# Which engine waits for the last stores: the final wait moved from SyncE to TensorE

## The chip, the cores and the metric

One core of one Trainium2 chip. The metric is the device time of one execution in microseconds (us), called the counted time where it stands beside the profiler's span of the same execution. A semaphore is a counter: in the traces here stores raise `stored` (three stores, 48 landings on semaphore 114), one instruction takes it down (159.633 us in the kernel before), and the kernel's waits test it. All runs told here are of the fast state, with a granted clock of 1.0.

## The reference

```python
def reference(x):                      # x: 32 x 512 x 1024 float32
    relu_x = np.maximum(x, 0)
    return np.sum(relu_x, axis=-1).astype(np.float32)
```

67 MB are read, 64 KB are written.

## The kernel before

The body streams the input through three buffers. ScalarE and VectorE clamp and sum, and SyncE issues every load and store. The last store carries two columns of results; each store raises the semaphore `stored` by 16 (the trace has 48 landings on it, the last at 159.599 us). What comes after the body:

```python
    n_stores = relu_sum(nc, sems, x, out)
    body.extend(ends)
    # ... (cut)
    nums = sorted(s.num for s in (*sems.loads, sems.act, sems.dve))
    cleared = range(nums[0], nums[-1] + 1)
    assert len(cleared) == len(nums)
    nc.sync.sem_clear(cleared)
    nc.sync.wait_ge(sems.stored, 16 * n_stores).then_inc(sems.stored, -16 * n_stores)
```

```python
    def store(m, n, act, dve):
        # ... (cut)
        nc.sync.wait_ge(sems.act, act)
        nc.sync.dma_start(out=dst, in_=src).wait_op(sems.dve, dve, "sem-ge").then_inc(
            sems.stored, 16
        )
        n_store += 1
```

So SyncE issues the third store (at 158.20 us), clears the semaphores of the body (99 to 113, at 158.57) while it flies, waits until `stored` (semaphore 114) is 48 (the last landing, 159.599), takes it down to zero (159.633), and leaves the program.

## Time and profile before

| | before |
|---|---|
| device time, first three runs | 161.35 us median (161.24 to 161.53) |
| the profiled execution, counted time | 160.99 us |
| its span, first to last instruction of the program | 159.63 us |
| its last store landed at | 159.599 us |

The page's span and the counted time are not the same thing: 1.36 us of the counted time lie after the program's last instruction. That stretch has no line in the page. It can be read only from the trace's record of semaphore updates.

### The profile page before, as it was taken

The page shows a single profiled execution, that of the slowest core. Times are in us where ns is not written, and L with a number is a line of the kernel's source. Part 1 is how long each engine was busy: PE and PEld are TensorE (multiplying, and loading weights), DVE is VectorE, ACT ScalarE, POOL GpSimd, SP SyncE. Part 2 cuts the span into 40 slices and gives each one's busy share as a digit, 9 for nine tenths or more (in the row PEclk, how much of TensorE's full clock was granted, in tenths as well). Part 3 has the DMA queues.
Part 4 walks back from the last instruction along what each step waited for, and adds up shares of the span by engine and source line. Part 5 has one row for each costly group of instructions (what it writes and reads, how often), then busy time and mean ns, then how long its engine had stood idle before and what let it go on. Part 6 is the DMA issues. An engine that isn't in the chain of part 4 may idle for free.

```text
span 159.6 us, 129 instructions
## 1 busy us (share of the span) xinstructions
DVE 117.5 (74%) x41; ACT 104.2 (65%) x50; POOL 0.2 (0%) x4
## 2 busy tenths in 40 slices
DVE  0000000009999499994999999999999999999986
ACT  3000059990799708996099941999339992499985
POOL 0000000000000000000000000000000000000000
DMA  7996996996996998979969969969969969798994
GB/s 263 525 525 263 525 526 263 525 525 263 526 493 296 525 411 378 525 328 460 526 279 509 525 263 526 525 263 525 525 263 525 509 279 525 337 452 386 412 405 127
DMA packets 2304, 67.18 MB, mean 421 GB/s; under 512 B 640, under 2 KB 896, under 8 KB 1024
## 3 DMA queue, kind: packets, MB, share of 16 engines
q1 hardware_dynamic: 2304, 67.18, 98.1%
HBM read 67.11 MB, written 0.07 MB: 421 GB/s over the span
## 4 chain that ended last, share of the span: by engine, by line
DMA 43%; DVE 34%; ACT 17%; another core or an unknown queue 3%; SPq 0%; issue 0%; DVEq 0%
DMA io<-in_x_dram 43%; DVE res L123 32%; ACT io L115 17%; DVE io L140 1%; SPq L97 0%; DVE piece L219 0%; DVE piece L140 0%; DVEq L218 0%
## 5 line engine op out<-in xcount | busy, mean ns | idle before, releaser
L123 DVE TENSOR_REDUCE res<-io 128x8 f32<-128x8192 f32 (+2 forms) x9 | 101.1, 11286 | 39.9 <-ACT io L115 39.9
L115 ACT ACTIVATE io<-io 128x8192 f32<-128x8192 f32 (+2 forms) x9 | 81.7, 9111 | 46.9 <-DMA io<-in_x_dram 46.9
L130 ACT ACTIVATE io<-io 128x1024 f32<-128x1024 f32 x20 | 20.9, 1045 | 5.9 <-DMA io<-in_x_dram 5.7
L140 DVE TENSOR_SCALAR_CACHE_REDUCE io<-io 128x1024 f32<-128x1024 f32 (+1 forms) x14 | 15.5, 1165 | 0.7 <-DMA io<-in_x_dram 0.6
L130 ACT ACTIVATION_READ_ACCUMULATOR io<-io 128x1 f32 x20 | 3.8, 188 | 0.0
L115 ACT ACT_TABLE_LOAD x1 | 1.3, 1283 | 0.8 <-PEq L260 0.8
L140 DVE DVE_READ_ACCUMULATOR io<-io 128x1 f32 x14 | 1.2, 82 | 0.0
L219 DVE TENSOR_SCALAR_CACHE_REDUCE piece<-piece 128x406 f32<-128x406 f32 x1 | 0.6, 576 | 0.1
L140 DVE TENSOR_SCALAR_CACHE_REDUCE piece<-piece 128x260 f32<-128x260 f32 x1 | 0.4, 424 | 0.0
L260 POOL MEMSET const-bfloat16-1.0<- 128x1 bf16 x1 | 0.1, 102 | 0.0
L260 POOL MEMSET const-uint8-127<- 128x1 uint8 x1 | 0.1, 102 | 0.0
L260 POOL MEMSET const-float32-0.0<- 128x1 f32 x1 | 0.1, 99 | 0.2 <-issue 0.2
L260 POOL MEMSET const-float32-1.0<- 128x1 f32 x1 | 0.1, 99 | 0.0
L140 DVE DVE_READ_ACCUMULATOR piece<-piece 128x1 f32 x1 | 0.1, 83 | 0.0
L219 DVE DVE_READ_ACCUMULATOR piece<-piece 128x1 f32 x1 | 0.1, 82 | 0.0
## 6 DMA issues: line engine op xcount, KB each, us to landing
io<-in_x_dram SPq DMA_DIRECT2D x1, 4096.0 KB, 21.6
io<-in_x_dram SPq DMA_DIRECT2D x1, 2048.0 KB, 26.1
io<-in_x_dram SPq DMA_DIRECT2D x1, 1204.0 KB, 28.6
io<-in_x_dram SPq DMA_DIRECT2D x1, 512.0 KB, 29.4
piece<-in_x_dram SPq DMA_DIRECT2D x1, 202.0 KB, 29.3
piece<-in_x_dram SPq DMA_DIRECT2D x1, 130.0 KB, 29.3
io<-in_x_dram SPq DMA_DIRECT2D x7, 26.9
out_dram<-res SPq DMA_DIRECT2D x1, 55.0 KB, 1.6
```

What stands on the lines that cost most here:

```text
L115: i = nc.scalar.activation(out=ap, in_=ap, func=RELU)
L123: nc.vector.tensor_reduce(out=res[:, m : m + n], in_=ap, axis=mybir.AxisListType.X, op=ADD).wait_op(sems.act, n_act, "sem-ge").then_inc(se ...
L130: i = nc.scalar.activation(out=ap, in_=ap, func=RELU, accum_out=res[:, m : m + 1])
L140: i = nc.vector.tensor_scalar(out=ap, in0=ap, scalar1=0.0, scalar2=None, op0=MAX, op1=ADD, accum_out=accum_out,)
L219: nc.vector.tensor_scalar(out=last[:, :], in0=last[:, :], scalar1=0.0, scalar2=None, op0=MAX, op1=ADD, accum_out=res[:, NT - 2 : NT - 1],) ...
L260: nc = _bacc.Bacc("TRN2", target_bir_lowering=False, num_devices=1)
```

## The change

The wait and the decrement move to TensorE, which has no busy line in this kernel's page. The apparent intent is that SyncE can go on to its own closing work while the last store is still in flight.

```diff
     nc.sync.sem_clear(cleared)
-    nc.sync.wait_ge(sems.stored, 16 * n_stores).then_inc(sems.stored, -16 * n_stores)
+    nc.tensor.wait_ge(sems.stored, 16 * n_stores).then_inc(sems.stored, -16 * n_stores)
     issue_ahead_of_the_barrier(tc, EARLY)
```

## The prediction

> **What bounds the kernel now.** I read the head of the page first, then the chain of work that ended last.
>
> ```profile
> span 159.6 us, 129 instructions
> DVE 117.5 (74%) x41; ACT 104.2 (65%) x50; POOL 0.2 (0%) x4
> q1 hardware_dynamic: 2304, 67.18, 98.1%
> HBM read 67.11 MB, written 0.07 MB: 421 GB/s over the span
> ...
> DMA 43%; DVE 34%; ACT 17%; another core or an unknown queue 3%; SPq 0%; issue 0%; DVEq 0%
> ```
>
> The reader is to see that the DMA engines are busy 98.1% of the span: the body is a stream of 67 MB, with VectorE and ScalarE behind it. TensorE has no busy line at all. The change touches no load, no arithmetic and no store, so I leave the body and look only at what follows the last arithmetic. The timeline gives the end of that, the list of DMA issues the flight of the last store, the DMA queue's own waits the wait that the change moves:
>
> ```profile
> 157.58 0.58 DVE L219 TENSOR_SCALAR_CACHE_REDUCE piece<-piece 128x406 f32<-128x406 f32 x1
> 157.62 0.19 ACT L130 ACTIVATION_READ_ACCUMULATOR io<-io 128x1 f32 x1
> 158.09 0.08 DVE L219 DVE_READ_ACCUMULATOR piece<-piece 128x1 f32 x1
> ...
> out_dram<-res SPq DMA_DIRECT2D x1, 1.0 KB, 1.4
> ...
> SPq L46 <- SPq L46: 1.0, 1, 1.0
> ...
> L46 SPq EVENT_SEMAPHORE  x1: 17/17/17, 159.6 to 159.6; - x1
> ```
>
> VectorE ends at 158.17 us; SyncE issues the last store at 158.20 (333 ns); that 1 KB lands 1.4 us after its issue. L46 is the wait for the stores; SyncE stands in it 1.0 us, it runs at 159.6, and with it the span ends. (L45, the clearing of the other semaphores, ran at 158.6 for 57 ns, beside the store's flight.) So after the last arithmetic the order is: store issue, flight of the store, wait released, end.
>
> The time that counts is longer than the span. The profiled execution has 160.99 us by the device and a span of 159.63: 1.36 us lie after the program's own last instruction. The trace also records every semaphore update[...]. In us from the span's start:
>
> ```
> semaphore 114 (stores)   last landing 159.599, taken down by SyncE 159.633
> semaphore 2, entering    1.003  157.912  157.950  158.313  159.764
> semaphore 2, returning   159.807 159.845 159.880 159.926
> semaphores 207-255 reset from 159.896, 156-206 from 159.946, 105-155 from 159.986,
>             54-104 from 159.990, 3-53 (first recorded is 7) from 160.140 to 160.488
> semaphore 2, second time 160.752 .786 .825 .869 .892 .990 161.028 .062 .109
> ```
>
> Semaphore 2 is passed along the engines and back. The late entries fit engine by engine the last update of each: ScalarE 157.812 then 157.912 (+100 ns), VectorE 158.180 then 158.313 (+133), SyncE 159.633 then 159.764 (+131). The one at 1.003 must be an engine that was done by then: TensorE (its one update at 0.784, +219) or GpSimd. I take TensorE as the first in line, because the block 3 to 53 is reset last and with a lag of about 0.19 us after its release, as long as the lag at 1.003. That is an inference; the record doesn't name the engine. Then the line is TensorE, ScalarE, GpSimd, VectorE, SyncE, and back. The sixth entry of the second round, 160.990 us, equals the device time of this execution, so I believe that the counted time ends inside this second round and everything that delays the first round is counted.
>
> [...]
>
> **The change part by part.** *Removed from SyncE:* a wait and decrement of 17 ns. SyncE still issues the store and clears 99 to 113, and then enters the closing line at about 158.63 + 0.13 = 158.76 instead of 159.764. This looks like a gain of 1 us but isn't: the line can't close before the store has landed, on whichever engine waits. *Added on TensorE:* the same wait. It sets no earlier release: the landing stays at 159.599.
>
> *Cost of one event-semaphore on TensorE.* The opening barrier shows it for both engines:
>
> ```profile
> L260 SPq EVENT_SEMAPHORE  x1: 17/17/17, 0.7 to 0.7; - x1
> ...
> L260 PEldq EVENT_SEMAPHORE  x1: 51/51/51, 0.7 to 0.7; - x1
> ```
>
> 51 ns against 17; from start to recorded update 63 against 18, so +45 ns. Landing to decrement was 34 ns on SyncE, so about 79 on TensorE: 159.678.
>
> *Leaving the program.* SyncE needed 131 ns from that update to its entry, TensorE 219 (0.784 to 1.003): entry at 159.897, against SyncE's 159.764.
>
> *The way through the line.* Before, the late engine was the one at the turn: only the four returning hops were left, 43 + 38 + 35 + 46 = 162 ns, and TensorE was released at 159.926. Afterwards the late engine is the first: four entering hops, 34 + 39 + 44 + 23 = 140 ns by the second round, then the turn at VectorE[...] (98 ns in the second round, 111 in an earlier one, against 43 where it had been waiting), then 38 + 34 + 47 = 119. With about 105 for the turn it is 140 + 105 + 119 = 364 ns: release at 159.897 + 0.364 = 160.261.
>
> *Sum.* 160.261 − 159.926 = +0.335 us, of it 45 for the slower instruction, 88 for the slower exit, 202 for the longer way. From there on TensorE resets its block, alone at the end, and opens the second round, before as after: nothing absorbs the delay. 161.35 + 0.335 = 161.69 us. I shade it to 161.65, because TensorE's 219 ns at the start need not repeat: with SyncE's 131 the sum is +0.25.
>
> **The rivals.**
> (a) *It gets faster by having SyncE free earlier.* This is probably the intent: the idle engine takes the wait, and SyncE's own closing work (its block 207 to 255) goes on early. Against it: SyncE's reset starts only when the line has turned at it (159.896, after its entry at 159.764), its block is done by 160.006, while block 3 to 53 ends at 160.488; SyncE isn't the last. If the order of the line were the other way round, TensorE would sit at the turn, and only 45 + 88 = +0.13 us would remain: 161.5.
> (b) *The counted time ends with SyncE's own last instruction plus a constant.* Then it falls by about a microsecond (SyncE's last instruction at 158.63 instead of 159.63): 160.35, −0.6%. For it: the metric is not defined in the profile. Against it: the 1.36 us after the span match an entry of the second round to the nanosecond, and that round needs all engines.
> (c) *TensorE, asleep since 0.8 us, wakes slowly or must fetch its next instructions.* [...] Against it: in the opening barrier it woke 13 ns after SyncE, and after a stand of 159 us in the closing line it began its reset within about 0.19 us.
> (d) *All hidden*: 161.35. Against it: in the first round nothing runs after the landing but the chain itself.
>
> **Range and chances.** The three runs before lie within 0.29 us (161.24 to 161.53), as much as the expected effect. Low end 161.35: the reversed line or a shorter exit, with a favourable draw. High end 161.95: the full sum with a slow wake and an unfavourable draw. A 2% verdict needs 3.2 us; even rival (b) gives a third of that. So within 2%: 0.98, and 0.01 on each side.
>
> **What would show it.** In the changed kernel's profile the wait's instruction should stand under PEldq with about 51 ns near 159.65, the span should be about the same or some 0.05 us longer, and SyncE's list should end with the clear at about 158.6. Among the semaphore updates three late entries should follow one at about 159.90 in hops of about 40 ns instead of standing at 157.9 to 158.3, and block 3 to 53 should begin about 0.33 us later after the last landing. If the counted time falls by a microsecond, rival (b) holds and I have the metric's end wrong; if late entries still stand at 157.9 and 158.3, I have the line's order wrong; if the wait starts well over 0.1 us after the last landing, it is (c).

The marks in this text stand for statements that no trace of this case shows. What the trace of the kernel before does show:

- Semaphore 2 is named by none of the program's 129 instructions. Its updates after the body, and the resets of the other semaphores, which come in five stretches of numbers (207, 156, 105, 54 and 3 upward), are called the closing sequence here; whose work it is the record doesn't say. That block 207 to 255 is SyncE's and block 3 to 53 TensorE's is inferred from the order in which they are reset.
- In the second round, nine updates again like the first, the hops are 23 to 47 ns, and the turn is 98. Why the turn takes 43 ns in the first round and 98 in the second isn't shown.
- The listing gives the wait's own instruction, not the time stood in it: SyncE stood 1.0 us at L46, which shows 17 ns.
- On rival (c): TensorE's event-semaphore is slower than the others' (51 ns against 17 to 21), and so is the exit taken to be its own (219 ns against 100 to 133). Its drain in the opening barrier is not: 8 ns, against 8 on ScalarE, 10 on VectorE, 132 on SyncE and 181 on GpSimd.

## The result, and the profile after

| | before | after |
|---|---|---|
| device time, six runs each | 161.34 us (161.16 to 161.53) | 161.61 us (161.48 to 161.84) |
| ratio of the fast runs | | 1.0018, interval 1.0005 to 1.0031 |
| the profiled execution, counted time | 160.99 us | 161.56 us |
| its last landing | 159.599 us | 159.814 us |
| counted time after the last landing | 1.391 us | 1.746 us |

A ratio is the mean time of one kernel's fast runs over that of the other's of the same rounds, so it is not quite the ratio of the medians. By it the changed kernel is about 0.29 us slower, which is "same" at the 2% level but clear of zero.

The page of the changed kernel, its head, its busy times and its DMA queue:

```profile
span 159.9 us, 129 instructions
...
DVE 117.5 (73%) x41; ACT 104.2 (65%) x50; POOL 0.2 (0%) x4
...
q1 hardware_dynamic: 2304, 67.18, 97.9%
```

The same number of instructions, the same busy times, the same bytes on this queue: the body was not touched. (This page also has one packet of 24 bytes on the queue of instructions, at 0.14 us; the kernel before has one like it 0.08 us ahead of its span.) The listing of the wait's own line, L46, and of the clear's, L45, in the changed kernel:

```profile
L46 PEldq EVENT_SEMAPHORE  x1: 51/51/51, 159.8 to 159.8; - x1
...
L45 SPq EVENT_SEMAPHORE_RANGE_CLEAR  x1: 58/58/58, 158.8 to 158.8; - x1
```

The wait now stands on TensorE's sequencer and shows 51 ns where SyncE's showed 17. The list of the DMA queue's own waits, changed kernel:

```profile
SPq L97 <- DVE res L123: 123.1, 5, 51.5
SPq L107 <- ACT io L130: 28.2, 2, 27.3
SPq L108 <- DVE piece L219: 0.3, 1, 0.3
SPq L260 <- PEq L260: 0.2, 1, 0.2
```

The line "SPq L46 <- SPq L46: 1.0, 1, 1.0" is gone, and nothing stands in its place in the lists of waits, this one or that of the engines. It is the same in the experiments below where the wait stands on ScalarE, GpSimd or VectorE, so it isn't that TensorE is idle; why the lists leave it out was not looked into. A reader of that list alone would book a gain of 1 us. In the DMA issues of the changed kernel the last store takes as long as before:

```profile
out_dram<-res SPq DMA_DIRECT2D x1, 1.0 KB, 1.4
```

The packet records split these 1.4 us: in the kernel before, 0.83 us pass from the start of the issue to the first packet, the packets take 0.20 us, and the last landing comes 0.38 us after the last packet; in the changed kernel it is 0.83, 0.20 and 0.37 us.

The semaphore record of the two executions shows where the time went. Times are in us from the span's start; "entering" and "returning" are the updates of semaphore 2, called the closing line:

```
                  before                                  after
last landing      159.599                                 159.814
114 taken down    159.633  (+34 ns)                       159.906  (+92)
entering          1.003 157.912 157.950 158.313 159.764   160.125 .159 .198 .242 .265
returning         159.807 .845 .880 .926                  160.363 .401 .435 .482
3-53 reset until  160.488                                 161.045
second round      160.752 .786 .825 .869 .892             161.310 .344 .383 .427 .450
                  .990 161.028 .062 .109                  .548 .586 .620 .667
counted time      160.990                                 161.560
```

Before, four engines had entered the line by 158.313 and only SyncE was late. After, nobody could enter until TensorE had, at 160.125, and the other four followed in hops of 34, 39, 44 and 23 ns. From the last landing to the last return it is 327 ns before and 668 ns after, 341 ns more. From that return to the opening of the second round it is 826 ns before and 828 after: nothing is made up.

The two profiled executions differ by 0.57 us in counted time, more than the kernels do. Of this, 0.215 us is a later last landing. The spans of the nine runs before in the first group of experiments lie between 159.7 and 159.9 us, so part of it at least is the variation of the body from run to run, and I don't read it as an effect of the change. The quantity free of it is the counted time after the last landing: 1.391 against 1.746 us.

That is one execution of each, but the record can check it on all. It gives every execution's time, and its span to 0.1 us. Time less span is 1.63 to 1.71 us in the six executions of the changed kernel, and 1.33 to 1.42 us in the 29 executions of the kernel before that were timed beside the experiments. The two ranges don't touch. (The span ends with the wait's own instruction, at 159.632 and 159.895 us in the two profiled executions, so this difference leaves out the few hundredths of a microsecond by which the semaphore is taken down later.)

### The profile page after: what moved, and what is told of

The parts are those of the page before. It is cut to its first block, busy times and chain, and to the rows that moved or that the text cites. A ratio compares the mean times of both kernels' runs of the same rounds, so it can differ in the third digit from the quotient of the medians.

```text
span 159.9 us, 129 instructions
## 1 busy us (share of the span) xinstructions
DVE 117.5 (73%) x41; ACT 104.2 (65%) x50; POOL 0.2 (0%) x4
## 4 chain that ended last, share of the span: by engine, by line
DMA 44%; DVE 33%; ACT 17%; another core or an unknown queue 3%; SPq 1%; issue 0%
DVE res L123 32%; DMA io<-in_x_dram 25%; DMA piece<-in_x_dram 18%; ACT io L115 17%; SPq L97 1%; DVE piece L219 0%
```

## The experiments

Each kernel gave the right result. In the tables, "landing to return" is from the last landing of a store to the last return of the closing line's first round, split in three: until the late engine has taken its semaphore down, until it has entered the line, and until the line has come back. It was 34 + 131 + 162 = 327 ns in the kernel before. "Tail" is the counted time after the last landing, less the 1.391 us of before.

### The wait on each of the engines

Edit, with `tensor`, `scalar`, `gpsimd` and `vector` in turn:

```diff
-    nc.sync.wait_ge(sems.stored, 16 * n_stores).then_inc(sems.stored, -16 * n_stores)
+    nc.scalar.wait_ge(sems.stored, 16 * n_stores).then_inc(sems.stored, -16 * n_stores)
```

Expected:

> The changed kernel again, on the chip where the next three run. Place theory (the late engine's place in the closing line counts, besides its own speed): from the last landing of a store to TensorE's release from the first round about 668 ns as in the first trace after, against 327 before; counted time +0.34 us (first result: +0.27 by the medians). Engine theory (TensorE's own slower instruction and exit are all of it, 45 + 88 ns, and the rest was chance): +0.13 us.

> ScalarE waits. Place theory (second in line): landing to decrement 34, exit 100, hops 39 + 44 + 23, turn 98, back 38 + 34 + 47: landing to last release about 457 ns, so +0.13 us. Engine theory: its exit of 100 ns against SyncE's 131 makes it -0.03 us. In the semaphore record the GpSimd, VectorE and SyncE entries should follow the late one, with one entry (TensorE) at about 1.0 us alone.

> GpSimd waits. Place theory (third in line): 34, an exit never seen alone, guessed as 131, hops 44 + 23, turn 98, back 119: about 449 ns, +0.12 us (up to +0.21 if its exit is as slow as TensorE's). Engine theory: about 0. In the record two entries, at about 1.0 us and after ScalarE's end, stand before the late one.

> VectorE waits. Place theory (fourth): 38, exit 133, hop 23, turn 98, back 119: about 411 ns, +0.08 us. Engine theory: about +0.01 us. In the record three early entries, then the late one and SyncE 23 ns behind it.

Measured, against 161.19 us for the kernel before on this chip (nine runs, 161.07 to 161.27):

| the wait is on | time, us | ratio (interval) | landing to return, ns | against before | tail, us |
|---|---|---|---|---|---|
| TensorE | 161.55 | 1.0024 (1.0011 to 1.0037) | 92 + 219 + 357 = 668 | +341 | +0.35 |
| ScalarE | 161.42 | 1.0015 (1.0001 to 1.0029) | 45 + 132 + 323 = 500 | +173 | +0.18 |
| GpSimd | 162.00 | 1.0046 (1.0034 to 1.0059) | 50 + 559 + 284 = 893 | +566 | +0.57 |
| VectorE | 161.33 | 1.0010 (0.9997 to 1.0022) | 58 + 172 + 243 = 473 | +146 | +0.16 |

Time less span, over all executions, is 1.65 to 1.70 us with TensorE, 1.50 to 1.53 with ScalarE, 1.90 to 1.98 with GpSimd and 1.48 to 1.54 with VectorE, against 1.33 to 1.42 for the nine of the kernel before. So the later end is in every execution, VectorE's too, and not in the profiled one alone.

The listing of L46 in the runs with the wait on TensorE's three alternatives, in the order GpSimd, VectorE, ScalarE, one fence each:

```profile
L46 POOLq EVENT_SEMAPHORE  x1: 17/17/17, 159.7 to 159.7; - x1
```

```profile
L46 DVEq EVENT_SEMAPHORE  x1: 21/21/21, 159.8 to 159.8; - x1
```

```profile
L46 ACTq EVENT_SEMAPHORE  x1: 17/17/17, 159.9 to 159.9; - x1
```

The instruction itself shows 17 to 21 ns on all three, as on SyncE, and all three make the kernel slower in their semaphore records (VectorE's ratio alone can't exclude zero). From landing to decrement they lose only 11 to 24 ns of their 146 to 566, so a slow instruction is not the main cause. The entries of semaphore 2 give the order away:

```
TensorE   160.161 .195 .233 .277 .300                   all five late
ScalarE   1.003   160.030 .069 .113 .136                 one early
GpSimd    0.993   157.982 160.281 .324 .347              two early
VectorE   0.996   158.094 158.132 160.013 .036           three early
SyncE     1.003   157.912 157.950 158.313 159.764        four early (the kernel before)
```

The line is TensorE, ScalarE, GpSimd, VectorE, SyncE. What the prediction had inferred from a lag is now shown: an engine that is late holds up all those behind it. The third term, which is nothing but the way through the line, falls in that order: 357, 323, 284, 243 and 162 ns. ScalarE shows it best: its first two terms together are 177 ns, 12 more than SyncE's 165, and the third makes up 161 of its +173.

The engine theory falls: it asked for -0.03 us with ScalarE and about 0 with GpSimd. The place theory holds in kind. Its sizes were too small, mostly because I had taken the way out of the program from engines that had come there from arithmetic. ScalarE took 132 ns from taking the semaphore down to its entry, not the 100 that it needs after its last sum (five traces), VectorE 172, not 133. Landing to decrement was underrated too, at 34 and 38 ns where it took 45 and 58. GpSimd's 559 ns was guessed as 131, and that is the one large miss; the next section but one takes it up. By the medians GpSimd's run is 0.81 us slower, of which the tail explains 0.57. The rest is in the span, whose mean over the five runs is 160.0 us against 159.8 before; I don't explain it.

### A wait on TensorE that isn't late

TensorE waits for the first two stores, on a semaphore of their own, and SyncE for the third:

```diff
-    nc.sync.wait_ge(sems.stored, 16 * n_stores).then_inc(sems.stored, -16 * n_stores)
+    nc.tensor.wait_ge(sems.early, 16 * (n_stores - 1)).then_inc(
+        sems.early, -16 * (n_stores - 1)
+    )
+    nc.sync.wait_ge(sems.stored, 16).then_inc(sems.stored, -16)
```

```diff
-            sems.stored, 16
+            sems.early if n_store < 2 else sems.stored, 16
```

> TensorE waits for the first two stores (own semaphore, taken down by it), SyncE for the third as before. Place theory: TensorE enters the line at about the second store's landing + 0.3 us, well over 0.5 us ahead of SyncE's entry, so nothing is late but SyncE: landing to last release 327 ns, counted time 0 against before (within 0.05). Rival (any wait on TensorE at the end costs, whatever its time[...]): +0.1 to +0.3 us.

Measured: 161.23 us median against 161.22, ratio 1.0006 (0.9993 to 1.0019). From landing to return it is 34 + 131 + 163 = 328 ns, as before. The lines of the two waits, in this run:

```profile
L46 PEldq EVENT_SEMAPHORE  x1: 51/51/51, 159.3 to 159.3; - x1
...
L49 SPq EVENT_SEMAPHORE  x1: 17/17/17, 160.5 to 160.5; - x1
```

TensorE took its semaphore down at 159.376 and entered at 159.595, 219 ns later, the same way out as in the changed kernel; SyncE entered at 160.697, 1.1 us later. So the slower instruction and the slower exit are there in full and cost nothing, since TensorE isn't the last. The rival that any wait on TensorE costs is out. (This profiled execution took 161.94 us, the slowest of the six. Its last landing was late, at 160.532 us; its tail was 1.408 us, like that of before. The delay lies in the body, and its cause is not known.)

### GpSimd's way out, off the path

The same split, with GpSimd in TensorE's place:

```diff
-    nc.tensor.wait_ge(sems.early, 16 * (n_stores - 1)).then_inc(
+    nc.gpsimd.wait_ge(sems.early, 16 * (n_stores - 1)).then_inc(
```

> GpSimd waits for the first two stores (own semaphore), SyncE for the third as before. The run in which GpSimd waited for all three showed 559 ns from its decrement to its entry, against 131 for SyncE, and the counted time rose by 0.74 us. If that is GpSimd's way out of the program as such, it shows again here, about 0.56 us between its decrement and the second entry behind ScalarE's or its own place in the record, but ends before SyncE's entry: counted time 0 against before (within 0.1), landing to last release 327 ns. If the 0.74 came from something that a wait on GpSimd does to the body (slower loads or VectorE), the counted time rises by some 0.2 us here too. If the 559 ns was a matter of that one execution, the exit here is about 130 to 220 ns.

Measured: 161.28 us against 161.25, ratio 0.9999 (0.9985 to 1.0012). GpSimd's semaphore went down at 158.784 us, its entry came at 159.343: 559 ns again, to the nanosecond. The lines of the two waits:

```profile
L46 POOLq EVENT_SEMAPHORE  x1: 17/17/17, 158.8 to 158.8; - x1
...
L49 SPq EVENT_SEMAPHORE  x1: 17/17/17, 160.0 to 160.0; - x1
```

SyncE entered at 160.175, and from landing to return it was 328 ns. So 559 ns is GpSimd's way out of the program in two kernels, and it is hidden when GpSimd is not the late one. What it consists of no record shows.

### Eight more waits, on either engine

```diff
+    for _ in range(8):
+        nc.tensor.wait_ge(sems.stored, 16 * n_stores)
-    nc.sync.wait_ge(sems.stored, 16 * n_stores).then_inc(sems.stored, -16 * n_stores)
+    nc.tensor.wait_ge(sems.stored, 16 * n_stores).then_inc(sems.stored, -16 * n_stores)
```

The second kernel adds the same eight to `nc.sync` and leaves the last wait there.

> TensorE waits, with eight more waits on the same value ahead of the last, which takes it down. If TensorE's slower exit (219 ns against 131) is some two ordinary sequencer steps at its slower pace (about 110 ns each against 62), then +8 x 0.11 = +0.9 us on top of the changed kernel's +0.3, so +1.2 against before. If a step costs only the 51 ns that the profile shows, +0.4 + 0.3 = +0.7. If the exit is slow for another cause (a fetch) and steps pass at SyncE's pace, +0.5 + 0.3 = +0.8.

> The kernel before with eight more satisfied waits on SyncE ahead of the last. By the pace in the trace before (a wait's start to the next instruction's start 83 ns, a DMA issue's end to the clear 45 ns, 17 ns of its own) about 62 ns each: +0.5 us against before, and none of it hidden, as the line's other engines have all entered.

The paces in these two are estimates from the trace before: about 110 ns is half of TensorE's 219, and 62 is 45 + 17.

Measured: 161.97 us with TensorE, ratio 1.0047 (1.0034 to 1.0059), and 161.48 us with SyncE, ratio 1.0016 (1.0004 to 1.0028), against 161.22. The listings of the waits' lines, first with TensorE, then with SyncE:

```profile
L47 PEldq EVENT_SEMAPHORE  x4: 51/51/51, 159.9 to 160.2; - x4
...
L48 PEldq EVENT_SEMAPHORE  x1: 51/51/51, 160.3 to 160.3; - x1
```

```profile
L47 SPq EVENT_SEMAPHORE  x4: 17/28/28, 159.7 to 159.9; - x4
...
L48 SPq EVENT_SEMAPHORE  x1: 28/28/28, 159.9 to 159.9; - x1
```

Count them: the nine waits became five instructions. By their operands in the trace the first holds one wait and each of the other four holds two, the last of them with the decrement. So four instructions were added and not eight, and the expected sums are to be halved: on TensorE, on top of the changed kernel, +0.9 becomes 0.44 in the first case, and about 0.2 and 0.25 in the two others; SyncE's +0.5 becomes 0.25. TensorE's instructions start 111, 106, 105 and 106 ns apart, together 428 ns; SyncE's 56, 64, 61 and 60, together 241 ns. (The first of these steps, 111 and 56 ns, is that of the instruction with a single wait, so holding two doesn't make the steps long.) From landing to return TensorE's kernel took 520 + 257 + 357 = 1134 ns, +807 against before and +466 against the changed kernel; SyncE's took 286 + 137 + 165 = 588 ns, +261. The tails are +0.77 and +0.27 us. TensorE's is 34 ns short of the +807: in this trace the second round opens 788 ns after the return, where it is 826 to 832 in the nine others, and that makes good the 38 ns of the longer exit. Neither is explained. So the first case holds for the pace, with the count of instructions mistaken.

Two things follow. A profile line of 51 ns stands for a step of about 107 ns on this path, and one of 17 to 28 ns for a step of about 60. And TensorE's way out of 219 ns against SyncE's 131 has about the same ratio (1.7) as the steps (107 against 60 ns, 1.8), as if both were two steps long. That is consistent with the first case of the expectation; the closing instructions themselves are not in the trace, so it isn't shown.

No experiment beat the kernel before. Its wait stands on the engine where the line turns, so the four others have entered before it (by 158.313 us, SyncE at 159.764) and only the way back is left (162 ns).

## Why the prediction was right

- **The place in the line.** Right, and it is the main part: predicted 202 ns, measured 357 - 162 = 195 ns. The 7 ns between them are the turn, taken as about 105 and measured as 98. Over the ten traces the hops are 23 to 48 ns, and the turn is 97 to 99 ns in the first round wherever SyncE isn't the late one, 43 to 45 where it is. The order of the engines was an inference, and a thin one: the two lags that the prediction calls equally long are about 0.19 and 0.22 us. The four runs with the wait moved along the line show that it is right.
- **The slower instruction.** Predicted +45 ns from landing to decrement, measured 92 - 34 = 58. The instruction showed 51 ns, as in the opening barrier; nearly all of the 13 ns that were missed are TensorE's later start, 30 ns after the landing against SyncE's 16.
- **The slower exit.** Predicted +88 ns, measured 219 - 131 = 88. TensorE's 219 ns came back in both executions of the changed kernel and in the one where TensorE waited for the first two stores. Only behind eight more waits was it 257, which I don't explain. I had shaded the time from 161.69 to 161.65 us for fear that the 219 would not repeat; that was needless. That 161.65 then lay nearer to the measured 161.61 than 161.69 would have is luck.
- **The sum.** 45 + 88 + 202 = 335 ns predicted, 58 + 88 + 195 = 341 ns measured. The timing gives about 0.29 us the first time, and 1.0024, about 0.39 us, on the second chip. Both intervals hold 0.34.
- **Where the counted time ends.** The prediction took it to end at the sixth entry of the second round, on the strength of one match that it calls exact to the nanosecond, though the device time is given in steps of 10 ns. In the nine later traces the counted time lies within 12 ns of that entry, so it does follow the second round. That it ends at this very entry isn't shown: the other entries of the round stand at nearly fixed distances from it, and where the counted time begins is not on record. Rival (b), a fall to 160.35 us, is out.
- **Rival (a), SyncE free earlier.** It was free, and it gained nothing: in the changed kernel its block of semaphores was reset from 160.394 us, 0.50 us later than before (0.28 if counted from the last landing). In both kernels that reset began only after the line's first return: 89 ns after it before (159.807), 31 ns after it in the changed kernel (160.363). Nor is that block the last: block 3 to 53 is the last to end in all ten traces, and the recorded resets run from 159.896 to 160.488 us before, 0.59 us, and for 0.65 us in the changed kernel. The reversed order that this rival allowed is out too.
- **Rival (c), a slow waking.** In the changed kernel the wait's instruction began 30 ns after the last landing, at 159.844 against 159.814. No waking of tenths of a microsecond is to be seen. Nor is a fetch: none of the ten traces records a packet on the queue of instructions after 0.18 us.

What I expected of the profile in clock times (the entry near 159.90, the clear near 158.6) came 0.2 us later, with the landing. Measured from the landing the entry came at 0.311 us where 0.298 was predicted, and block 3 to 53 began 0.34 us later than before where 0.33 was.

## What to carry to other kernels

Ask of a final wait not which engine is idle but which engine the rest of the launch needs last. In this launch the engines leave through a line that starts at TensorE and turns at SyncE, so of the five places tried the last wait is cheapest on SyncE (327 ns from landing to return), and an idle engine early in the line (TensorE, 668 ns) is the dearest place but for one with a slow exit (GpSimd, 893 ns, of it 559 for the exit). An idle engine's wait was free only where another engine was later still (328 ns, with TensorE 1.1 us and GpSimd 0.83 us ahead of SyncE), and when a wait vanishes from a list of waits, look for where it has gone before booking a gain.
